# A streaming Huber loss on one core: from bf16 intermediates on three queues to fp32 in place, with every transfer issued by SyncE

## The chip, the cores and the metric

The kernel runs on one core of a Trainium2 chip. The metric is device microseconds of one execution, lower is better. Before the change the median of three runs is 1923.24 us (1923.15 to 1923.33). One further execution was recorded by the hardware profiler; all durations below come from it.

## The reference

Two inputs of 8192x8192 fp32 give one output of the same shape and type:

```python
def reference(pred, target):
    delta = 1.0
    diff = pred - target
    abs_diff = np.abs(diff)
    return np.where(abs_diff <= delta, 0.5 * diff**2, delta * (abs_diff - 0.5 * delta))
```

With c = clip(diff, -1, 1) this is c²/2 + relu(|diff| - 1), which is what both kernels compute. Per element two fp32 numbers are read and one is written: 536.87 MB in and 268.44 MB out.

## The kernel before

The rows are cut into 64 tiles of 128 rows (one row per partition). A tile has 8192 columns, so an input tile is 4 MB (4096 KB), and one tile of work moves 12.58 MB (805.3 MB over 64).

**Loads.** `emit_loads(i)` (lines 46 to 58) loads each input tile in two halves of 4096 columns, 2048 KB and 16 KB rows each. Both halves of `pred` and the first half of `target` are issued from SyncE (SP), the second half of `target` from ScalarE (ACT) (L54, L56). There are three buffers each for `a` (pred) and `b` (target), each half a tile wide.

**Work.** In the main loop (tiles 0 to 61) GpSimd (POOL) subtracts the halves into a bf16 tile `dfull` (L103), ACT takes the absolute value in place (L108), VectorE (DVE) writes min(|d|, 1) into the bf16 tile `sfull` (L109), and one tile later `do_tail` squares `sfull` on ACT with a scale (L68), applies relu(|d| - 1) on ACT (L69) and adds the two on DVE (L70). Each of these but the subtraction is one instruction over 128x8192 elements.

**Stores.** `flush` issues one 4096 KB store per tile from POOL's queue (L63), which turns bf16 into fp32 on the way.

**End.** The last two tiles are cut into pieces of 2048 and 1024 columns (lines 120 to 228). Their pieces use DVE forms that the main loop does not have, among them L147 (scalar_tensor_tensor, two tensors in), L152 (tensor_tensor) and L154 (tensor_scalar) over 128x2048.

**What sets the order.** Each engine runs its own instruction list strictly in order and waits on semaphores. The list is not simply the order of the Python source: the tile framework plans it from dependencies and its own estimates when the program is built. Each load waits on its issuing engine until its buffer is released.

Of the kernel before, what the change touches and what calls it, by code (L numbers as in the profile page):

```python
# [9 lines left out]
def kernel(  # L10
# [6 lines left out]
    nc = tc.nc  # L17
    P = 128
    fp32 = mybir.dt.float32
    bf16 = mybir.dt.bfloat16  # L20
    Alu = mybir.AluOpType
    Act = mybir.ActivationFunctionType

    n_rows, n_cols = pred.shape
    COLS = 4096
    n_ct = n_cols // COLS
    SQRT_HALF = 0.70710678118654752
# [6 lines left out]
    neg1 = nc.alloc_sbuf_tensor("huber_neg1_bf16", [P, 1], bf16)  # L34
# [4 lines left out]
    pool_d = ctx.enter_context(tc.tile_pool(name="sbuf_d", bufs=2))  # L39
    pool_s = ctx.enter_context(tc.tile_pool(name="sbuf_s", bufs=3))  # L40

    loads = {}
    pending_tail = []
    pending_store = []

    def emit_loads(i):
        if i >= n_rt:
            return
        tl = []
        for j in range(n_ct):  # L50
            c0 = j * COLS
            a = pool_a.tile([P, COLS], fp32)
            b = pool_b.tile([P, COLS], fp32)
            nc.sync.dma_start(out=a, in_=pred_t[i, :, c0 : c0 + COLS])  # L54
            beng = nc.sync if j == 0 else nc.scalar
            beng.dma_start(out=b, in_=targ_t[i, :, c0 : c0 + COLS])  # L56
            tl.append((a, b))
        loads[i] = tl

    def flush(limit):  # L60
        while len(pending_store) > limit:
            r, pi = pending_store.pop(0)
            nc.gpsimd.dma_start(out=out_t[pi, :, :], in_=r)  # L63

    def do_tail(limit):
        while len(pending_tail) > limit:
            s, d, pi = pending_tail.pop(0)
            nc.scalar.activation(out=s, in_=s, func=Act.Square, scale=SQRT_HALF)  # L68
            nc.scalar.activation(out=d, in_=d, func=Act.Relu, bias=neg1.ap())  # L69
            nc.vector.tensor_tensor(out=s, in0=s, in1=d, op=Alu.add)  # L70
            pending_store.append((s, pi))

    def act_path(d, s):
        nc.scalar.activation(out=d, in_=d, func=Act.Abs)
        nc.vector.tensor_scalar(
            out=s, in0=d, scalar1=1.0, scalar2=None, op0=Alu.min
        )
        nc.scalar.activation(out=s, in_=s, func=Act.Square, scale=SQRT_HALF)
        nc.scalar.activation(out=d, in_=d, func=Act.Relu, bias=neg1.ap())
        nc.vector.tensor_tensor(out=s, in0=s, in1=d, op=Alu.add)  # L80

    def dve_path(d, s):
        nc.vector.tensor_scalar(
            out=s, in0=d, scalar1=-1.0, scalar2=1.0, op0=Alu.max, op1=Alu.min
        )
        nc.vector.scalar_tensor_tensor(
            out=d, in0=s, scalar=-0.5, in1=d, op0=Alu.mult, op1=Alu.add
        )
        nc.vector.tensor_tensor(out=s, in0=s, in1=d, op=Alu.mult)

    emit_loads(0)
    for i in range(n_rt - 2):
        dfull = pool_d.tile([P, n_cols], bf16)
        sfull = pool_s.tile([P, n_cols], bf16)

        emit_loads(i + 1)

        do_tail(0)

        for j in range(n_ct):  # L100
            c0 = j * COLS
            a, b = loads[i][j]
            nc.gpsimd.tensor_tensor(  # L103
                out=dfull[:, c0 : c0 + COLS], in0=a, in1=b, op=Alu.subtract
            )
        del loads[i]

        nc.scalar.activation(out=dfull, in_=dfull, func=Act.Abs)  # L108
        nc.vector.tensor_scalar(  # L109
            out=sfull, in0=dfull, scalar1=1.0, scalar2=None, op0=Alu.min,  # L110
        )

        flush(1)

        pending_tail.append((sfull, dfull, i))

    i62 = n_rt - 2
    i63 = n_rt - 1
    H = n_cols // 2

    d62 = pool_d.tile([P, n_cols], bf16, tag="dfull")
    s62 = pool_s.tile([P, n_cols], bf16, tag="sfull")

    emit_loads(i63)
    do_tail(0)

    for j in range(n_ct):
        c0 = j * COLS
        a, b = loads[i62][j]
        nc.gpsimd.tensor_tensor(  # L130
            out=d62[:, c0 : c0 + COLS], in0=a, in1=b, op=Alu.subtract
        )
    del loads[i62]

    flush(1)

    Q = 2048
    dq = [d62[:, k * Q : (k + 1) * Q] for k in range(4)]
    sq = [s62[:, k * Q : (k + 1) * Q] for k in range(4)]
    nc.scalar.activation(out=dq[0], in_=dq[0], func=Act.Abs)  # L140
    nc.vector.tensor_scalar(out=sq[0], in0=dq[0], scalar1=1.0, scalar2=None, op0=Alu.min)  # L141
    nc.vector.tensor_scalar(  # L142
        out=sq[1], in0=dq[1], scalar1=-1.0, scalar2=1.0, op0=Alu.max, op1=Alu.min
    )
    nc.scalar.activation(out=sq[0], in_=sq[0], func=Act.Square, scale=SQRT_HALF)  # L145
    nc.scalar.activation(out=dq[0], in_=dq[0], func=Act.Relu, bias=neg1.ap())
    nc.vector.scalar_tensor_tensor(  # L147
        out=dq[1], in0=sq[1], scalar=-0.5, in1=dq[1], op0=Alu.mult, op1=Alu.add
    )
    nc.vector.tensor_tensor(out=sq[0], in0=sq[0], in1=dq[0], op=Alu.add)  # L150
    nc.scalar.activation(out=dq[2], in_=dq[2], func=Act.Abs)
    nc.vector.tensor_tensor(out=sq[1], in0=sq[1], in1=dq[1], op=Alu.mult)  # L152
    nc.vector.tensor_scalar(out=sq[2], in0=dq[2], scalar1=1.0, scalar2=None, op0=Alu.min)  # L153
    nc.vector.tensor_scalar(  # L154
        out=sq[3], in0=dq[3], scalar1=-1.0, scalar2=1.0, op0=Alu.max, op1=Alu.min
    )
    nc.scalar.activation(out=sq[2], in_=sq[2], func=Act.Square, scale=SQRT_HALF)  # L157
    nc.scalar.activation(out=dq[2], in_=dq[2], func=Act.Relu, bias=neg1.ap())  # L158
    nc.vector.scalar_tensor_tensor(  # L159
        out=dq[3], in0=sq[3], scalar=-0.5, in1=dq[3], op0=Alu.mult, op1=Alu.add  # L160
    )
    nc.vector.tensor_tensor(out=sq[2], in0=sq[2], in1=dq[2], op=Alu.add)  # L162
    nc.vector.tensor_tensor(out=sq[3], in0=sq[3], in1=dq[3], op=Alu.mult)

    d63 = pool_d.tile([P, n_cols], bf16, tag="dfull")
    s63 = pool_s.tile([P, n_cols], bf16, tag="sfull")

    bounds = [0, 2048, 4096, 6144, 7168, 8192]
    chunks = [(bounds[k], bounds[k + 1]) for k in range(len(bounds) - 1)]

    flush(0)
    for k, (lo, hi) in enumerate(chunks):
        a, b = loads[i63][lo // COLS]
        o0, o1 = lo % COLS, (hi - 1) % COLS + 1
        nc.gpsimd.tensor_tensor(  # L175
            out=d63[:, lo:hi], in0=a[:, o0:o1], in1=b[:, o0:o1], op=Alu.subtract
        )
        if 1 <= k <= 4:
            nc.gpsimd.dma_start(  # L179
                out=out_t[i62, :, (k - 1) * Q : k * Q], in_=sq[k - 1]  # L180
            )
    del loads[i63]

    d0, s0 = d63[:, 0:2048], s63[:, 0:2048]
    d1, s1 = d63[:, 2048:4096], s63[:, 2048:4096]
    d2, s2 = d63[:, 4096:6144], s63[:, 4096:6144]
    d3, s3 = d63[:, 6144:7168], s63[:, 6144:7168]
    d4, s4 = d63[:, 7168:8192], s63[:, 7168:8192]

    def st(lo, hi, s):  # L190
        nc.gpsimd.dma_start(out=out_t[i63, :, lo:hi], in_=s)  # L191

    nc.scalar.activation(out=d0, in_=d0, func=Act.Abs)
    nc.vector.tensor_scalar(out=s0, in0=d0, scalar1=1.0, scalar2=None, op0=Alu.min)  # L194
    nc.scalar.activation(out=s0, in_=s0, func=Act.Square, scale=SQRT_HALF)  # L195
    nc.scalar.activation(out=d0, in_=d0, func=Act.Relu, bias=neg1.ap())
    nc.vector.tensor_scalar(
        out=s1, in0=d1, scalar1=-1.0, scalar2=1.0, op0=Alu.max, op1=Alu.min
    )
    nc.vector.scalar_tensor_tensor(  # L200
        out=d1, in0=s1, scalar=-0.5, in1=d1, op0=Alu.mult, op1=Alu.add
    )
    nc.vector.tensor_tensor(out=s1, in0=s1, in1=d1, op=Alu.mult)
    st(2048, 4096, s1)
    nc.vector.tensor_tensor(out=s0, in0=s0, in1=d0, op=Alu.add)
    st(0, 2048, s0)
    nc.scalar.activation(out=d2, in_=d2, func=Act.Abs)
    nc.vector.tensor_scalar(out=s2, in0=d2, scalar1=1.0, scalar2=None, op0=Alu.min)
    nc.scalar.activation(out=s2, in_=s2, func=Act.Square, scale=SQRT_HALF)
    nc.scalar.activation(out=d2, in_=d2, func=Act.Relu, bias=neg1.ap())  # L210
    nc.vector.tensor_scalar(
        out=s4, in0=d4, scalar1=-1.0, scalar2=1.0, op0=Alu.max, op1=Alu.min
    )
    nc.vector.scalar_tensor_tensor(
        out=d4, in0=s4, scalar=-0.5, in1=d4, op0=Alu.mult, op1=Alu.add
    )
# [40 lines left out]
```

## Time and profile before

| Quantity | Value |
|---|---|
| median of three runs | 1923.24 us |
| span of the profiled execution | 1921.5 us |
| median less that span (the time around it) | 1.74 us |
| data moved over the span | 805.42 MB, mean 419 GB/s |
| DVE busy | 851.1 us (44%) |
| ACT busy | 1326.3 us (69%) |
| POOL busy | 1289.1 us (67%) |

"Busy" counts an engine's own work. The span runs from the first to the last instruction. A group row reads: line, engine, operation, tiles and shapes, count, then busy time in us and the mean duration of one in ns. A timeline row reads: start in us, duration in us, engine, line, operation. The windows view gives busy time of each engine in a stretch, and for the transfers their busy share (over 1.00 where packets of two queues overlap on an engine) and GB/s.

### The profile page before, as it was taken

What the parts mean: (1) busy time and instruction counts of PE and PEld (TensorE: products, weight loads), DVE (VectorE), ACT (ScalarE), POOL (GpSimd) and SP (SyncE); (2) the same over time, 40 slices, a digit from 0 to 9 for tenths busy, and PEclk for the clock granted to TensorE, in tenths of its full rate; (3) what the DMA queues carried; (4) which work ended last, traced back from release to release, by engine and by line L of the source; (5) the groups of instructions that cost most, each with busy time, mean ns of one, the idle gap of its engine ahead of it and who ended that gap; (6) DMA issues with size and microseconds to landing.
All of it is one profiled execution on the core that took longest, in us unless ns stands there. A gap on an engine that the chain in (4) does not pass through costs nothing.

```text
span 1921.5 us, 1430 instructions
## 1 busy us (share of the span) xinstructions
DVE 851.1 (44%) x146; ACT 1326.3 (69%) x202; POOL 1289.1 (67%) x207
## 2 busy tenths in 40 slices
DVE  0344354453443534534435345344353443544566
ACT  2866767668677676686776866767768667676674
POOL 5686676766866767667677676676766866767664
DMA  9999999999999999999999999999999999999996
GB/s 404 378 415 426 425 428 425 422 424 426 424 426 424 426 423 426 423 427 424 427 422 425 424 426 422 428 424 425 422 425 427 424 424 423 425 424 424 426 432 269
DMA packets 47099, 805.42 MB, mean 419 GB/s; under 512 B 5232, under 2 KB 5232, under 8 KB 5488
## 3 DMA queue, kind: packets, MB, share of 16 engines
q1 hardware_dynamic: 27648, 402.67, 54.0%
q0 software_dynamic: 10224, 268.44, 32.9%
q10 hardware_dynamic: 9216, 134.22, 16.3%
q14 instruction: 11, 0.09, 0.0%
HBM read 536.87 MB, written 268.44 MB: 419 GB/s over the span
## 4 chain that ended last, share of the span: by engine, by line
ACT 51%; DVE 29%; issue 18%; DMA 1%; POOL 1%; ACTq 0%; POOLq 0%; SPq 0%
DVE sfull L109 28%; ACT dfull L108 23%; ACT sfull L68 22%; ACT dfull L69 5%; DMA b<-in_target_dram 1%; POOL dfull L103 1%; DVE s_1188 L153 1%; DVE s_1188 L142 0%; DVE sfull L70 0%; DVE s_1220 L194 0%; DVE d_1187 L147 0%; DVE d_1187 L159 0%; ACT d_1187 L158 0%; ACT s_1220 L195 0%; ACTq L252 0%
## 5 line engine op out<-in xcount | busy, mean ns | idle before, releaser
L103 POOL TENSOR_TENSOR dfull<-a,b 128x4096 bf16<-128x4096 f32 x124 | 1213.8, 9803 | 588.0 <-issue 558.8
L68 ACT ACTIVATE sfull<-sfull 128x8192 bf16<-128x8192 bf16 x62 | 435.9, 7030 | 532.8 <-DVE sfull L109 532.8
L70 DVE TENSOR_TENSOR sfull<-sfull,dfull 128x8192 bf16<-128x8192 bf16 x62 | 274.4, 4426 | 860.6 <-ACT dfull L69 860.6
L109 DVE TENSOR_SCALAR sfull<-dfull 128x8192 bf16<-128x8192 bf16 x62 | 528.7, 8528 | 194.9 <-ACT dfull L108 194.9
L108 ACT ACTIVATE dfull<-dfull 128x8192 bf16<-128x8192 bf16 x62 | 434.8, 7013 | 33.2 <-POOL dfull L103 33.2
L69 ACT ACTIVATE dfull<-dfull,huber_neg_bf 128x8192 bf16<-128x8192 bf16 x62 | 440.6, 7106 | 0.0
L63 POOL DMA_DIRECT2D out_dram<-sfull x62 | 35.8, 577 | 3.8 <-DVE sfull L70 3.8
L130 POOL TENSOR_TENSOR d_1187<-a,b 128x4096 bf16<-128x4096 f32 x2 | 19.6, 9836 | 9.5 <-issue 9.5
L175 POOL TENSOR_TENSOR d_1219<-a,b 128x2048 bf16<-128x2048 f32 (+1 forms) x5 | 18.1, 3643 | 0.1
L191 POOL DMA_DIRECT2D out_dram<-s_1220 x5 | 2.7, 541 | 11.7 <-DVE s_1220 L217 5.9
L153 DVE TENSOR_SCALAR s_1188<-d_1187 128x2048 bf16<-128x2048 bf16 x1 | 9.8, 9846 | 0.0
L142 DVE TENSOR_SCALAR s_1188<-d_1187 128x2048 bf16<-128x2048 bf16 x1 | 9.3, 9318 | 0.0
L179 POOL DMA_DIRECT2D out_dram<-s_1188 x4 | 2.2, 553 | 10.5 <-DVE s_1188 L152 4.2
L195 ACT ACTIVATE s_1220<-s_1220 128x2048 bf16<-128x2048 bf16 x1 | 1.9, 1910 | 8.1 <-DVE s_1220 L194 8.1
L162 DVE TENSOR_TENSOR s_1188<-s_1188,d_1187 128x2048 bf16<-128x2048 bf16 x1 | 6.1, 6057 | 2.7 <-ACT d_1187 L158 2.7
L157 ACT ACTIVATE s_1188<-s_1188 128x2048 bf16<-128x2048 bf16 x1 | 1.9, 1910 | 6.0 <-DVE s_1188 L153 6.0
L145 ACT ACTIVATE s_1188<-s_1188 128x2048 bf16<-128x2048 bf16 x1 | 1.9, 1910 | 4.1 <-DVE s_1188 L141 4.1
L194 DVE TENSOR_SCALAR s_1220<-d_1219 128x2048 bf16<-128x2048 bf16 x1 | 3.3, 3278 | 0.0
L147 DVE SCALAR_TENSOR_TENSOR d_1187<-s_1188,d_1187 128x2048 bf16<-128x2048 bf16 x1 | 2.3, 2293 | 0.0
L159 DVE SCALAR_TENSOR_TENSOR d_1187<-s_1188,d_1187 128x2048 bf16<-128x2048 bf16 x1 | 2.3, 2284 | 0.0
L200 DVE SCALAR_TENSOR_TENSOR d_1219<-s_1220,d_1219 128x2048 bf16<-128x2048 bf16 x1 | 2.3, 2280 | 0.0
L108 ACT ACT_TABLE_LOAD x1 | 1.3, 1283 | 1.2 <-PEq L241 1.2
(32 smaller groups left out, 34.7 us busy)
## 6 DMA issues: line engine op xcount, KB each, us to landing
a<-in_pred_dram SPq DMA_DIRECT2D x128, 2048.0 KB, 18.1
out_dram<-sfull POOLq DMA_DIRECT2D x62, 4096.0 KB, 20.1
b<-in_target_dram ACTq DMA_DIRECT2D x64, 2048.0 KB, 13.9
b<-in_target_dram SPq DMA_DIRECT2D x64, 2048.0 KB, 25.3
out_dram<-s_1188 POOLq DMA_DIRECT2D x4, 1024.0 KB, 7.9
out_dram<-s_1220 POOLq DMA_DIRECT2D x3, 1024.0 KB, 4.1
out_dram<-s_1220 POOLq DMA_DIRECT2D x2, 512.0 KB, 5.0
```

The costliest lines, as they stand in the source:

```text
L63: nc.gpsimd.dma_start(out=out_t[pi, :, :], in_=r)
L68: nc.scalar.activation(out=s, in_=s, func=Act.Square, scale=SQRT_HALF)
L69: nc.scalar.activation(out=d, in_=d, func=Act.Relu, bias=neg1.ap())
L70: nc.vector.tensor_tensor(out=s, in0=s, in1=d, op=Alu.add)
L103: nc.gpsimd.tensor_tensor(out=dfull[:, c0 : c0 + COLS], in0=a, in1=b, op=Alu.subtract)
L108: nc.scalar.activation(out=dfull, in_=dfull, func=Act.Abs)
L109: nc.vector.tensor_scalar(out=sfull, in0=dfull, scalar1=1.0, scalar2=None, op0=Alu.min,)
L130: nc.gpsimd.tensor_tensor(out=d62[:, c0 : c0 + COLS], in0=a, in1=b, op=Alu.subtract)
L142: nc.vector.tensor_scalar(out=sq[1], in0=dq[1], scalar1=-1.0, scalar2=1.0, op0=Alu.max, op1=Alu.min)
L153: nc.vector.tensor_scalar(out=sq[2], in0=dq[2], scalar1=1.0, scalar2=None, op0=Alu.min)
L162: nc.vector.tensor_tensor(out=sq[2], in0=sq[2], in1=dq[2], op=Alu.add)
L175: nc.gpsimd.tensor_tensor(out=d63[:, lo:hi], in0=a[:, o0:o1], in1=b[:, o0:o1], op=Alu.subtract)
```

## The change

The intermediates in bf16, the POOL work and the separate tiles `dfull` and `sfull` go. There are three slots each for `a` and `b`, each a whole fp32 tile of 128x8192 (rows of 32 KB), and all work is done in place in them:

- `load(i)` issues one 4096 KB load for `a` and one for `b`, `store(i)` one 4096 KB store of `b`, all from SP, in the fixed order: loads of tile i, then the store of tile i-2. Only the last tile's `target` load and store are cut into four of 1024 KB. The store moves fp32 to fp32.
- `chunk` treats 2048 columns at a time, four per tile: DVE subtracts into `a` (L68), DVE clips into `b` (L69), ACT squares `b` with the scale (L72), takes the absolute value of `a` (L73) and relu(|d| - 1) of `a` (L74). `add` (L65) adds `a` into `b` on DVE; the source calls it two chunks later.
- A load of tile i+3 can only start when its slots are free: `a` when tile i's last add is done, `b` when tile i's store has landed.

```diff
+    CH = 2048
+    n_ch = n_cols // CH
-    pool_d = ctx.enter_context(tc.tile_pool(name="sbuf_d", bufs=2))
-    pool_s = ctx.enter_context(tc.tile_pool(name="sbuf_s", bufs=3))
+    def load(i):
+        a = pool_a.tile([P, n_cols], fp32)
+        nc.sync.dma_start(out=a, in_=pred_t[i, :, :])
+        b = pool_b.tile([P, n_cols], fp32)
+        pieces = n_ch if i == n_rt - 1 else 1
+        w = n_cols // pieces
+        for k in range(pieces):
+            nc.sync.dma_start(
+                out=b[:, k * w : (k + 1) * w], in_=targ_t[i, :, k * w : (k + 1) * w]
+            )
+        return a, b
+    def store(i, b):
+        pieces = n_ch if i == n_rt - 1 else 1
+        w = n_cols // pieces
+        for k in range(pieces):
+            nc.sync.dma_start(
+                out=out_t[i, :, k * w : (k + 1) * w], in_=b[:, k * w : (k + 1) * w]
+            )
+    flight = []
+    def add(a, b):
+        nc.vector.tensor_tensor(out=b, in0=b, in1=a, op=Alu.add)
+    def chunk(a, b):
+        nc.vector.tensor_tensor(out=a, in0=a, in1=b, op=Alu.subtract)
         nc.vector.tensor_scalar(
-            out=s, in0=d, scalar1=1.0, scalar2=None, op0=Alu.min
+            out=b, in0=a, scalar1=-1.0, scalar2=1.0, op0=Alu.max, op1=Alu.min
         )
+        nc.scalar.activation(out=b, in_=b, func=Act.Square, scale=SQRT_HALF)
+        nc.scalar.activation(out=a, in_=a, func=Act.Abs)
+        nc.scalar.activation(out=a, in_=a, func=Act.Relu, bias=neg1.ap())
+        flight.append((a, b))
+        if len(flight) > 2:
+            add(*flight.pop(0))
+    tiles = {}
+    for i in range(n_rt + 2):
+        if i < n_rt:
+            tiles[i] = load(i)
+        if i == n_rt:
+            while flight:
+                add(*flight.pop(0))
+        if i >= 2:
+            store(i - 2, tiles.pop(i - 2)[1])
+        if i < n_rt:
+            a, b = tiles[i]
+            for k in range(n_ch):
+                sl = slice(k * CH, (k + 1) * CH)
+                chunk(a[:, sl], b[:, sl])
...
-    emit_loads(0)
-    for i in range(n_rt - 2):
...
```

When the program is built, the planner fixes the lists of the engines. From the fourth tile to the last they repeat, per tile (chunks 0 to 3):

```
DVE: L68 c0, L68 c1, L69 c0, L69 c1, L68 c2, L68 c3, L69 c2, L69 c3, L65 c0, L65 c1, L65 c2, L65 c3
ACT: L72 c0, L73 c0, L72 c1, L74 c0, L73 c1, L72 c2, L74 c1, L73 c2, L72 c3, L74 c2, L73 c3, L74 c3
```

In tiles 0 to 2 the lists of neighbouring tiles are interleaved: on DVE the first clip of tile 1 stands behind the third add of tile 0, and the subtractions of tile 2 behind the third add of tile 1.

More of the change, by code (lines that the diff above doesn't have):

```diff
@@ L19 @@
     fp32 = mybir.dt.float32
-    bf16 = mybir.dt.bfloat16
     Alu = mybir.AluOpType
     Act = mybir.ActivationFunctionType
+    SQRT_HALF = 0.70710678118654752
     n_rows, n_cols = pred.shape
-    COLS = 4096
-    n_ct = n_cols // COLS
-    SQRT_HALF = 0.70710678118654752
+    CH = 2048
+    n_ch = n_cols // CH
     pred_t = pred.rearrange("(n p) m -> n p m", p=P)
@@ L32 @@
     n_rt = pred_t.shape[0]
-    neg1 = nc.alloc_sbuf_tensor("huber_neg1_bf16", [P, 1], bf16)
+    neg1 = nc.alloc_sbuf_tensor("huber_neg1", [P, 1], fp32)
     nc.gpsimd.memset(neg1.ap(), -1.0)
@@ L38 @@
     pool_b = ctx.enter_context(tc.tile_pool(name="sbuf_b", bufs=3))
-    pool_d = ctx.enter_context(tc.tile_pool(name="sbuf_d", bufs=2))
-    pool_s = ctx.enter_context(tc.tile_pool(name="sbuf_s", bufs=3))
[L42 to L71, printed above, removed]
@@ L73, in act_path @@
-    def act_path(d, s):
-        nc.scalar.activation(out=d, in_=d, func=Act.Abs)
+    def load(i):
[9 more added lines that the diff above has]
+        return a, b
@@ L77, in act_path @@
         )
[L78 to L89, printed above, removed]
@@ L91 @@
-    emit_loads(0)
-    for i in range(n_rt - 2):
[L93 to L216, printed above, removed]
-    nc.vector.tensor_tensor(out=s2, in0=s2, in1=d2, op=Alu.add)
@@ L218 @@
-    st(4096, 6144, s2)
-    nc.scalar.activation(out=d3, in_=d3, func=Act.Abs)
-    nc.vector.tensor_scalar(out=s3, in0=d3, scalar1=1.0, scalar2=None, op0=Alu.min)
-    nc.scalar.activation(out=s3, in_=s3, func=Act.Square, scale=SQRT_HALF)
-    nc.scalar.activation(out=d3, in_=d3, func=Act.Relu, bias=neg1.ap())
-    nc.vector.tensor_tensor(out=s4, in0=s4, in1=d4, op=Alu.mult)
-    st(7168, 8192, s4)
-    nc.vector.tensor_tensor(out=s3, in0=s3, in1=d3, op=Alu.add)
-    st(6144, 7168, s3)
+        nc.scalar.activation(out=b, in_=b, func=Act.Square, scale=SQRT_HALF)
```

## The prediction

> **What bounds the kernel now.** I read the page's busy line and its slices of transfer first, then windows, then the tail of the timeline for the prices of single instructions.
>
> ```profile
> span 1921.5 us, 1430 instructions
> DVE 851.1 (44%) x146; ACT 1326.3 (69%) x202; POOL 1289.1 (67%) x207
> ...
> DMA  9999999999999999999999999999999999999996
> GB/s 404 378 415 426 425 428 425 422 424 426 424 426 424 426 423 426 423 427 424 427 422 425 424 426 422 428 424 425 422 425 427 424 424 423 425 424 424 426 432 269
> ```
>
> No engine is busy over 69%; the transfers are busy in every slice. Windows: a stretch at the start with loads alone, 31 periods of the main loop, the end.
>
> ```profile
> 0.00:5.00 5.00, 0.00 (x0) 1.28 (x1) 0.31 (x5) 1.00 0.66 229
> 5.00:30.00 25.00, 0.00 (x0) 0.00 (x0) 11.94 (x2) 1.00 1.01 432
> 103.70:1022.33 918.63, 403.94 (x63) 649.83 (x93) 624.98 (x94) 1.00 1.04 425
> 1882.00:1921.50 39.50, 24.64 (x15) 17.83 (x11) 16.09 (x11) 1.00 0.61 234
> ```
>
> The last two columns are the transfers' busy share and GB/s. The main loop takes 918.63/31 = 29.63 us per tile for 12.58 MB, with the transfers at share 1.04: transfers set its pace. Loads alone, nearly all on one queue, reach 432 GB/s. The end loses: 39.5 us at 234 instead of 425 GB/s is 18 us lost.
>
> ```profile
> 1863.46 2.29 DVE L147 SCALAR_TENSOR_TENSOR d_1187<-s_1188,d_1187 128x2048 bf16<-128x2048 bf16 x1
> 1865.67 0.69 DVE L154 TENSOR_SCALAR s_1188<-d_1187 128x2048 bf16<-128x2048 bf16 x1
> 1866.27 1.22 DVE L152 TENSOR_TENSOR s_1188<-s_1188,d_1187 128x2048 bf16<-128x2048 bf16 x1
> ...
> 1896.10 3.28 DVE L194 TENSOR_SCALAR s_1220<-d_1219 128x2048 bf16<-128x2048 bf16 x1
> ...
> 1899.41 1.91 ACT L195 ACTIVATE s_1220<-s_1220 128x2048 bf16<-128x2048 bf16 x1 [8.13 <-DVE s_1220 L194]
> 1901.23 1.99 ACT L196 ACTIVATE d_1219<-d_1219,huber_neg_bf 128x2048 bf16<-128x2048 bf16 x1
> ...
> 1903.12 1.89 ACT L207 ACTIVATE d_1219<-d_1219 128x2048 bf16<-128x2048 bf16 x1
> ...
> 1904.92 1.04 ACT L219 ACTIVATE d_1219<-d_1219 128x1024 bf16<-128x1024 bf16 x1
> ```
>
> To be seen: prices at 2048 columns, and start to start. Square to relu 1.82 us, relu to abs 1.89, abs to next 1.80 (an independent successor starts about 0.1 before the end). On DVE L147 to L154 is 2.21 for a 2.29. DVE to ACT costs 0.03 (L194 ends 1899.38, L195 starts 1899.41).
>
> **Part 1, transfers.** Bytes are the same. Removed: POOL's converting stores and ACT's loads; five transfers per tile become three. Bounds per tile: 12.58/0.432 = 29.1 us (loads alone), 12.58/0.425 = 29.6 (the mixed loop). I take 29.4: the new queue also holds one kind at a time, but a third of it is stores, whose plain fp32 form no row shows; the converting stores ran inside the 425. Transfers alone would thus give 2.3 us lost at the start (5 us at 229 instead of 432 GB/s is 2.35), 64 x 29.4 = 1881.6, and an end of 5 us after the last byte, 1889 us of span. That would be faster.
>
> Size gains nothing here: two loads of 2 MB in a row already run at 432 GB/s. The Trainium skill, DMA: Bandwidth & Descriptors, section "Anatomy of one DMA — SWDGE (gpsimd) path", gives about 2.0 us fixed plus bytes at 436 GB/s per transfer. If that were paid in series, two transfers fewer would save an estimated 4 us per tile; the 432 GB/s window shows that queued transfers hide it.
>
> **Part 2, the loop through DVE and ACT.** The compiled lists decide this. From the fourth tile on, DVE does a tile's four adds directly ahead of the next tile's first subtraction, although the source calls them two chunks later. The last add waits for ACT's last relu of that tile; ACT's first square of the next tile waits for that tile's first clip, which stands behind two subtractions. So one tile's chain is closed before the next begins, whatever is already loaded:
>
> - two subtractions, start to start 2 x 2.21 = 4.42;
> - one clip 1.22, and 0.03 to ACT: ACT starts at 5.67;
> - ACT: four squares, abs and relus, 4 x (1.82 + 1.80 + 1.89) = 22.04. The last relu stands directly behind the abs that it needs and cannot overlap it: 0.12 more; its full 1.99 counts: 0.10 more. ACT ends at 27.93;
> - 0.03 to DVE, and the last add, start to start 2.21: 30.17; my count with the overlaps that the rows give is 30.1.
>
> Everything else (clips and subtractions of chunks 2 and 3, adds 0 to 2) lies beside ACT, whose 22.04 us cover them: 4.42 + 3 x 1.14 + 3 x 2.21 = 14.5 us of DVE. If that cover went, DVE's whole 4 x (2.21 + 1.14 + 2.21) = 22.2 us would still be under 29.4.
>
> Unseen prices. fp32 subtract and add on DVE: the bf16 tensor_tensor is 1.22 (L152), the only fp32 row is POOL's L175, 4.5 us at 2048 columns. I take 2.29: L147 also reads two tensors at one element per step, and 1.22 with twice the bytes less its fixed 0.16 (1.22 against 0.69 at 1024, L223) comes to 2.28. At 1.22 the loop would be 26.9, under the transfers; at 4.5 it would be 36.8. fp32 clip: between 0.69 (L154, bf16) and 2.29 (L147); by bytes 0.69 x 2 less 0.16 is 1.22, the value taken. At 0.69 the loop is 29.6, at 2.29 it is 31.2. ACT in fp32: its time grows by 0.83 ns per element from 2048 (1.91) to 8192 (7.03), and DVE's L152 takes bytes out of the same memory faster, so elements and not bytes set it; unchanged is the value, twice is the far end (by bytes, 52 us a tile), a gain I exclude since fewer bytes did not make the bf16 pace.
>
> The Trainium skill, VectorE: DVE Perf Modes, section "The perf-mode tier table (the rule you actually need)", prices fp32 tensor_tensor at 2293 ns and fp32 tensor_scalar at 1227 ns for 2048 elements, twice their bf16 prices: a rule against this change. By its figures the loop is an estimated 30.1 to 30.2, as by the rows; at the rows' far ends it is 26.9 or 36.8. No row of this trace shows either form.
>
> **Part 3, the waits on SP.** SP issues load i, then store i-2; a waiting store holds the later loads. After tile j's last add, SP issues store j and the load of `a` for j+3; the load of `b` waits for store j to land: 9.8 us of transfer and some 2 to land, while `a` itself takes 9.8 behind the store. Then `b` is in about 31 us after the add; tile j+3 begins two loops, 60 us, after it. This costs nothing while the loop is the longer. If it is not, the cover is `a`'s 9.8 us against a landing of 2. POOL's work goes: 67% busy, off the path. With it goes DVE's slow clip beside POOL (8.53 us, against 3.85 in the first tile, at 42.72): L109 is in the chain of work with 28%, but the transfers set that pace, so I price it at nothing.
>
> **Part 4, start and end.** Tile 0 is complete at about 22.2 (2.35 + 8.39 MB at 0.432 = 21.8, plus an estimated 0.4 until the semaphore is seen). ACT starts 5.67 later, at 27.9, and runs through tiles 0 and 1 without a hole, since the planner mixes them: 22.1 for tile 0, 22.6 for tile 1, whose four relus each stand directly behind their abs (22.04 + 4 x 0.12 + 0.10), so to 72.6. Tile 2's subtractions start behind tile 1's third add, which follows its third relu at 67.0: at 69.2. Tile 2 ends at 69.2 + 30.1 = 99.3. Then 61 tiles at 30.1 follow: 1835.4 (61 x 30.09), last add at 1935. After it the last 1024 KB store: before, from the last store's issue at 1912.66 to the end were 8.8 us (bounds: landings took 4.1 to 5.1; the rest is closing), so 1944 of span. The end no longer loses 18 us of transfer, but the chain, not transfers, ends last.
>
> **Sum.** 99.3 + 1835.4 + 8.8 = 1943.5, rounded up to 1944 of span, against the profiled 1921.5. Around it lie 1923.24 - 1921.5 = 1.74 us. Predicted: 1946 us, 1.2% slower.
>
> **Rivals.**
> - *Transfers set the pace, faster.* If ACT does not go empty between tiles (a chip order or prices that close the chain under 29.4), the time is 1889 + 1.7 = 1891. It decides from a loop of 30.1 - 23/61 = 29.7 on, only 0.4 us under mine. For it: DVE and ACT need only 22 us each. Against: the lists are fixed, and ACT's 22.04 are measured. With a clip of 0.69 alone: 29.6 x 61 gives 1914.
> - *The clip or the chain is dearer.* A clip of 2.29 lengthens the loop by 1.07 and the first tiles by 7.7: 1946 + 65 + 7 = 2018. For it: no fp32 clip is shown. Against: the bytes.
> - *One ring cannot keep the pace.* With loads and stores in one order, each change of kind could leave a gap. From 0.7 us per tile on it decides (12.58 MB in 30.1 is 418 GB/s); 1 us per transfer gives 29.4 + 3 = 32.4 x 64 + 10 = 2084. Against: 432 GB/s across several loads in a row.
> - *The change does less than it says.* A 32 KB row may still be cut into smaller packets; with 16 KB rows already at 432 GB/s this is worth nothing.
>
> **How the numbers follow.** Chances: my loop 0.73 (its own range 1932 to 1962, a quarter microsecond a tile either way), transfers pacing or a cheap clip 0.13, a dear clip 0.09, the ring 0.05. Leaving out the 1891 case, the 2084 case and the end of the dear clip gives 1910 to 1985, about 8 in 10. A measurement of this kernel tells 0.2% from no change, that is 1919.4 to 1927.1. Slower: 0.73 + 0.09 + 0.05 less a sliver, 0.85; the same 0.03; faster 0.12.
>
> **What would show it.** Right: ACT busy about 22 x 64 = 1400 us, idle some 8 us once per tile before the square, waiting for the clip; the last add waiting for ACT; transfers near 418 GB/s with SP waiting on DVE; clip rows of 1.2 us. Wrong: transfers at 425 or more throughout and SP stalled only on landings (the first rival); clip rows near 2.3; fp32 subtraction rows far from 2.29; or ACT rows over 2 us, which would make all of it longer.

## The result, and the profile after

The changed kernel takes 1943.91 us (median of four, 1943.79 to 1943.94) against 1923.20 us for the kernel before: a ratio of 1.0108, 95% interval 1.0093 to 1.0122. It is slower, by about 20.7 us. The profiled execution has a span of 1942.2 us.

The page of the changed kernel: head, GB/s in 40 equal slices of the span, shares of the chain of work that ended last, groups:

```profile
span 1942.2 us, 2040 instructions
...
DVE 1435.1 (74%) x768; ACT 1421.5 (73%) x769; POOL 0.3 (0%) x5
...
GB/s 413 429 431 432 431 433 432 431 434 435 432 433 430 427 413 420 423 411 421 421 410 422 420 411 422 418 422 412 416 421 415 421 420 411 421 420 421 411 367 173
...
ACT 73%; DVE 19%; issue 7%; DMA 1%; DVEq 0%; SPq 0%
...
L65 DVE TENSOR_TENSOR b<-b,a 128x2048 f32<-128x2048 f32 x256 | 586.2, 2290 | 479.4 <-ACT a L74 479.4
L72 ACT ACTIVATE b<-b 128x2048 f32<-128x2048 f32 x256 | 485.8, 1898 | 488.5 <-DVE b L69 488.5
L68 DVE TENSOR_TENSOR a<-a,b 128x2048 f32<-128x2048 f32 x256 | 574.4, 2284 | 22.9 <-DMA b<-in_target_dram 22.9
L74 ACT ACTIVATE a<-a,huber_neg 128x2048 f32<-128x2048 f32 x256 | 509.5, 1990 | 2.2
L73 ACT ACTIVATE a<-a 128x2048 f32<-128x2048 f32 x256 | 484.7, 1894 | 0.0
L69 DVE TENSOR_SCALAR b<-a 128x2048 f32<-128x2048 f32 x256 | 301.7, 1219 | 0.0
```

Three readings matter. First, the idle columns: ACT's square (L72) waited 488.5 us for DVE's clip, and DVE's add (L65) waited 479.4 us for ACT's relu. The two engines wait for each other. Neither is busy over 74%, and DVE waited for a load only once, 22.9 us at the very start. Second, the chain that ended last: 73% of the span are ACT's work, 19% DVE's, 1% transfers. Third, the GB/s row: up to the 13th slice the transfers run at about 432 GB/s, and SP waits almost only for landings of stores (280 us between 100 and 400 us, against 22 us for DVE's adds); from the 15th on they fall to 410 to 423, because they are now held back to the pace of the work (between 1000 and 1900 us SP waits 525 us for the adds, 328 for landings).

One period of the loop, in the timeline of the changed kernel (start, duration, engine, line):

```profile
911.00 2.29 DVE L65 TENSOR_TENSOR b<-b,a 128x2048 f32<-128x2048 f32 x1 [1.54 <-ACT a L74]
913.22 4.49 DVE L68 TENSOR_TENSOR a<-a,b 128x2048 f32<-128x2048 f32 x2
...
917.62 2.35 DVE L69 TENSOR_SCALAR b<-a 128x2048 f32<-128x2048 f32 x2
918.87 1.91 ACT L72 ACTIVATE b<-b 128x2048 f32<-128x2048 f32 x1 [7.90 <-DVE b L69]
...
939.09 2.00 ACT L74 ACTIVATE a<-a,huber_neg 128x2048 f32<-128x2048 f32 x1
941.12 2.29 DVE L65 TENSOR_TENSOR b<-b,a 128x2048 f32<-128x2048 f32 x1 [1.54 <-ACT a L74]
943.33 2.28 DVE L68 TENSOR_TENSOR a<-a,b 128x2048 f32<-128x2048 f32 x1
```

To be seen: the period is 943.33 - 913.22 = 30.11 us. From the first subtraction to ACT's first square 5.65 us, ACT from 918.87 to 941.09, 22.22 us without a hole, then 0.03 and the last add's 2.21 until the next tile's subtraction can start. ACT stands idle 7.90 us once per tile, between its last relu and the next tile's first clip, though the next tile's data is there: after the start DVE waits for no load.

What SP waited for, in the changed kernel (who waited, for whom, us in total, times, longest; L46 issues the load of `b`, L55 the store):

```profile
SPq L46 <- DMA out_dram<-b: 917.6, 61, 28.1
SPq L55 <- DVE b L65: 916.5, 65, 32.0
```

These are the two longest waits of the whole trace and cost nothing here, as the experiment with half the stores shows below: SP waits because it is early.

The transfers' busy share does not show who sets the pace. A late stretch in the changed kernel, and then the same in the source-order kernel below, which does wait for its loads (the last two columns are busy share and GB/s):

```profile
1022.00:1850.00 828.00, 615.40 (x329) 608.48 (x330) 0.00 (x0) 1.00 1.00 418
```

```profile
1022.00:1850.00 828.00, 645.37 (x343) 643.14 (x342) 0.00 (x0) 1.00 1.00 431
```

Both have 1.00: in the changed kernel, whose transfers are held back, some packet records are longer (a 32 KB row takes 1239 ns in the mean against 1217 in the source-order run, with a median of 1213 in both). So the share of 1.04 in the kernel before does not by itself show that transfers set its pace, as the prediction reads it; no run tested that.

The kernel before spends 29.63 us per tile, this one 30.12 ((1907.14 - 100.01)/60 from the first subtractions of the last and the fourth tile). Over 61 periods that is 30 us more; some 9 us of it come back at the two ends, which I did not separate.

### The profile page after: what moved, and what is told of

It is laid out like the page before. It is cut to its first block, busy times and chain, and to the rows that moved or that the text cites. A ratio compares the mean times of both kernels' runs of the same rounds, so it can differ in the third digit from the quotient of the medians.

```text
span 1942.2 us, 2040 instructions
## 1 busy us (share of the span) xinstructions
DVE 1435.1 (74%) x768; ACT 1421.5 (73%) x769; POOL 0.3 (0%) x5
## 4 chain that ended last, share of the span: by engine, by line
ACT 73%; DVE 19%; issue 7%; DMA 1%; DVEq 0%; SPq 0%
ACT a L74 25%; ACT b L72 24%; ACT a L73 24%; DVE a L68 15%; DVE b L69 4%; DMA b<-in_target_dram 1%; DVE b L65 0%; DVEq L69 0%; SPq L41 0%; DVEq L68 0%
## 5 line engine op out<-in xcount | busy, mean ns | idle before, releaser
L65 DVE TENSOR_TENSOR b<-b,a 128x2048 f32<-128x2048 f32 x256 | 586.2, 2290 | 479.4 <-ACT a L74 479.4
L72 ACT ACTIVATE b<-b 128x2048 f32<-128x2048 f32 x256 | 485.8, 1898 | 488.5 <-DVE b L69 488.5
L68 DVE TENSOR_TENSOR a<-a,b 128x2048 f32<-128x2048 f32 x256 | 574.4, 2284 | 22.9 <-DMA b<-in_target_dram 22.9
L74 ACT ACTIVATE a<-a,huber_neg 128x2048 f32<-128x2048 f32 x256 | 509.5, 1990 | 2.2
L73 ACT ACTIVATE a<-a 128x2048 f32<-128x2048 f32 x256 | 484.7, 1894 | 0.0
L69 DVE TENSOR_SCALAR b<-a 128x2048 f32<-128x2048 f32 x256 | 301.7, 1219 | 0.0
```

What stands on the lines that cost most here:

```text
L65: nc.vector.tensor_tensor(out=b, in0=b, in1=a, op=Alu.add)
L68: nc.vector.tensor_tensor(out=a, in0=a, in1=b, op=Alu.subtract)
L69: nc.vector.tensor_scalar(out=b, in0=a, scalar1=-1.0, scalar2=1.0, op0=Alu.max, op1=Alu.min)
L72: nc.scalar.activation(out=b, in_=b, func=Act.Square, scale=SQRT_HALF)
L73: nc.scalar.activation(out=a, in_=a, func=Act.Abs)
L74: nc.scalar.activation(out=a, in_=a, func=Act.Relu, bias=neg1.ap())
```

## The experiments

### The order of DVE and ACT alone

The edit leaves work, transfers and buffers as they are and only asks the planner to keep the order of the source on DVE and ACT:

```diff
+    keep = tc.keep_in_program_order
-        nc.vector.tensor_tensor(out=b, in0=b, in1=a, op=Alu.add)
+        keep(nc.vector.tensor_tensor(out=b, in0=b, in1=a, op=Alu.add))
-        nc.vector.tensor_tensor(out=a, in0=a, in1=b, op=Alu.subtract)
+        keep(nc.vector.tensor_tensor(out=a, in0=a, in1=b, op=Alu.subtract))
...
```

The clip and ACT's three instructions are wrapped in the same way.

> Same work, transfers and waits as the changed kernel, but DVE and ACT keep the order of the source: a tile's last two adds come after the first two subtractions and clips of the next tile. Theory (the closed chain subtract, subtract, clip, ACT, add sets 30.1 us a tile): the chain opens, DVE needs 4 x (2.32 + 1.14 + 2.21) = 22.7 and ACT 4 x (1.82 + 1.92 + 1.89) = 22.5 us a tile, so transfers pace it at the 431 to 436 GB/s of the changed kernel's early slices: 12.58/0.432 = 29.1 a tile, 1870 to 1890 us in all, faster than the kernel before (1923). Rival (one ring with loads and stores in turn gives only the 412 to 420 GB/s of the later slices): 1925 to 1945, as the changed kernel.

Measured: 1875.21 us, ratio to the kernel before 0.975 (0.9734 to 0.9767); 68.7 us less than the changed kernel. The slices and waits of this run, whose lines stand one further down (L69 subtracts, L70 clips, L73 squares, L75 is the relu, L66 the add):

```profile
span 1873.9 us, 2040 instructions
...
GB/s 414 425 435 430 432 432 433 430 435 432 432 435 432 432 434 432 432 434 434 430 434 435 429 434 434 430 433 434 432 432 434 431 432 432 431 435 432 413 433 367
```

```profile
DVE a L69 <- DMA b<-in_target_dram: 409.2, 62, 22.8
ACT b L73 <- DVE b L70: 385.2, 61, 7.9
...
DVE b L66 <- ACT a L75: 1.4, 1, 1.4
```

The GB/s row no longer falls. DVE now waits for a load on nearly every tile (409.2 us, 62 times) and for ACT once, 1.4 us: the transfers set the pace. (ACT still waits for the clip, 385.2 us, because the clip waits for the load.) The theory holds, and the rival that one ring (a single queue, here SP's) with loads and stores in turn is limited to 412 to 420 GB/s falls. This version beats both kernels.

### One clip moved forward

Here the adds still stand ahead of the next tile; only the subtractions of chunks 1 to 3 are held behind the clip of chunk 0, which `first` keeps. (The planner then moved two more things, as the trace shows: the first add ahead of the fourth subtraction, and ACT's relu of chunk 0 ahead of its square of chunk 1.)

```diff
+        if k >= 1:
+            with tc.issue_after(first[-1].ins):
+                nc.vector.tensor_tensor(out=a, in0=a, in1=b, op=Alu.subtract)
```

> Only one thing of DVE's order is changed: the clip of a tile's first chunk stands directly behind its subtraction, ahead of the subtractions of the other chunks. Adds still come ahead of the next tile. Theory: the chain loses one subtraction, 30.1 - 2.2 + 0.1 = 28.0 us, which is under the transfers' 29.1, so transfers take over and it ends where the source order does plus the last tile's tail, 1870 to 1895 us. If each microsecond of chain counted without a floor it would be 1943 - 2.1 x 61 = 1815. Rival (ring): 1925 to 1945.

Measured: 1876.57 us, ratio 0.9758 (0.9743 to 0.9773). The waits of this run (L74 is the first subtraction):

```profile
DVE a L74 <- DMA b<-in_target_dram: 65.6, 50, 22.8
```

Shortening the chain by one subtraction is enough: DVE now waits for a load 50 times. The gain stops at the transfers, as expected, and not at the 1815 us that the chain alone would give.

### The same dose in two places

A second, idle clip per tile: once for chunk 0, where it stands in the chain, once for chunk 3, where it stands beside ACT. The twin has `k == 3` in the same place. ACT's order of squares and abs is pinned so that the planner does not rearrange it.

```diff
+        if k == 0:
+            nc.vector.tensor_scalar(
+                out=b, in0=b, scalar1=-1.0, scalar2=1.0, op0=Alu.max, op1=Alu.min
+            )
```

> The changed kernel with a second, idle clip for the first chunk of every tile; on DVE it stands behind the clip of the second chunk, so ACT's first square waits 2 x 1.14 = 2.28 us longer. ACT keeps its order. Theory (closed chain): period 30.12 + 2.28 = 32.40, 61 periods give 139 us more, 2075 to 2090 us. Rival (DVE's or ACT's total work, or transfers, set the period): DVE has 7 us of holes per tile, so no change, 1944.

> The same second clip, but for the last chunk of every tile, where it stands behind the first add, ahead of a hole of DVE. The same DVE work is added as in the twin. Theory (closed chain): it lies beside ACT and costs nothing, 1940 to 1950 us. Rival (total work of DVE counts): as much as the twin, 2010 to 2090 us.

Measured: 2084.08 us in the chain (ratio 1.0837, 1.0815 to 1.0858), 1944.36 us beside it (ratio 1.0110, 1.0090 to 1.0130). The first run's line of waits for ACT and the second's (L78 squares, L70 clips, L74 is the second clip):

```profile
ACT b L78 <- DVE b L74: 629.0, 64, 10.2
```

```profile
ACT b L78 <- DVE b L70: 488.1, 63, 7.9
```

In the chain, ACT's wait grows from 7.9 to 10.2 us per tile, by the expected 2.28 of two clips (the second clip of chunk 0, and chunk 1's, behind which it stands); beside ACT it stays. The same added DVE work costs 140 us in one place and 0.5 in the other. Total work does not set the time, the closed chain does.

### Half the stores

```diff
-        w = n_cols // pieces
+        w = n_cols // pieces if i == n_rt - 1 else n_cols // 2
```

> Stores of all tiles but the last cover only columns 0 to 4095; the rest of the output is not written. All compute stays. One sixth of the bytes goes. Theory (chain): no change against the changed kernel, 1940 to 1946 us, period 30.1. Rival (transfers or landings of stores set the pace, since the loads of b wait 918 us in total for stores): down by up to a sixth of the transfers, 1640 to 1900 us.

Measured: 1936.44 us, ratio 1.0069 (1.0054 to 1.0084). A sixth of the bytes less, and 7.5 us less: neither the 0 to 4 of the theory nor anything like the rival's 44 to 300. The transfers are at share 0.85 in the middle of this run, SP's wait for landings of stores falls from 917.6 to 54.3 us, and the period stays: subtractions start at 913.22 and 943.34, as in the changed kernel to 0.01 us. The 7.5 us are at the end:

```profile
1895.64 2.29 DVE L65 TENSOR_TENSOR b<-b,a 128x2048 f32<-128x2048 f32 x1 [2.95 <-ACT a L74]
1897.85 2.29 DVE L68 TENSOR_TENSOR a<-a,b 128x2048 f32<-128x2048 f32 x1
1901.13 2.29 DVE L65 TENSOR_TENSOR b<-b,a 128x2048 f32<-128x2048 f32 x1 [1.00 <-ACT a L74]
1903.34 1.22 DVE L69 TENSOR_SCALAR b<-a 128x2048 f32<-128x2048 f32 x1
```

In this build the planner put the last tile's first subtraction and clip ahead of the last adds of the tile before. One of the 61 places where the chain closes between two tiles is gone (ACT waits 62 times instead of 63), and each costs 7.9 us of ACT's time. So the run misses its expectation by a change of order that I had not looked for, and that change is a small copy of the first experiment.

### Transfers by themselves

All compute left out; the stores write the loaded target.

```diff
-                chunk(a[:, sl], b[:, sl])
+                pass
```

> All compute is left out; what is stored is the loaded target. The loads and stores, their order and their slots stay. It prices the transfers by themselves. Theory: 805.3 MB at 432 GB/s is 1864, with start and end 1870 to 1880 us. Rival (ring slower by itself): 1925 or more.

Measured: 1870.53 us, ratio 0.9727 (0.9707 to 0.9746). One ring moves loads and stores in turn at 432 to 433 GB/s (windows 103 to 1022 and 1022 to 1850 us). The source-order kernel is 4.7 us above this floor.

### Stores from POOL's queue, and rows of 16 KB

Both start from the source-order kernel and undo one part of the change in its transfers. The first issues the stores, in `store`, from POOL:

```diff
-            nc.sync.dma_start(
+            nc.gpsimd.dma_start(
                 out=out_t[i, :, k * w : (k + 1) * w], in_=b[:, k * w : (k + 1) * w]
             )
```

> The source-order kernel with its stores issued from POOL's queue instead of SP's; still fp32 to fp32, no conversion. It undoes one part of the change and asks what raised the transfers from 425 GB/s (kernel before) to 432. Theory: the stores' own path through POOL cost it; with it the main loop falls back to 425 GB/s, 1900 to 1910 us. Rival (the path is free; the conversion, or 16 KB rows, or the mixing by two more queues cost it): 1873 to 1880 us.

The second loads `a`, and `b` in the same way, in halves:

```diff
-        nc.sync.dma_start(out=a, in_=pred_t[i, :, :])
+        for k in range(2):
+            nc.sync.dma_start(
+                out=a[:, k * 4096 : (k + 1) * 4096],
+                in_=pred_t[i, :, k * 4096 : (k + 1) * 4096],
+            )
```

> The source-order kernel with every load of a and b cut into two halves of 4096 columns, 16 KB rows and 2048 KB each, as the kernel before had them; all still from SP. In the traces a 16 KB row takes 611 ns on its transfer engine (kernel before), a 32 KB row 1213 (source-order run). Theory (the row length itself has a price): 32 x 611 - 16 x 1213 = 0.14 us a tile, and two more transfers with their completions, estimated from nothing to 0.1; 64 tiles give 9 to 16 us, 1884 to 1891 us. Rival (row length is free, POOL's queue made all the difference): 1875 to 1877 us.

Measured: 1905.05 us with POOL's stores (1898.99 to 1906.36; ratio 0.9898, 0.9879 to 0.9916), 1885.43 us with halves (ratio 0.9801, 0.9783 to 0.9818). So stores from POOL's queue cost 30 us (24 to 31 over the four runs) and loads in halves 10 us against 1875.21. The windows of the POOL run (us, busy of DVE, ACT and POOL, clock, transfers' share, GB/s):

```profile
103.00:1022.00 919.00, 714.80 (x381) 712.66 (x379) 17.05 (x32) 1.00 1.00 429
1022.00:1850.00 828.00, 626.27 (x333) 626.25 (x333) 14.39 (x27) 1.00 1.00 424
```

Against 432 and 431 in the same windows of the source-order run. The 10 us fit the packet records: a 16 KB row takes 611 ns (median) on its transfer engine in the kernel before and 612 in this run, a 32 KB row 1213, so 32 x 611 - 16 x 1213 = 144 ns a tile (176 with 612), 9 to 11 us over 64. Halves are also twice as many loads; the packets alone account for the difference, but rows and number of loads were not tried apart.

For POOL's queue the median packet shows no price: there too a 32 KB row takes 1213 ns. By the windows about 20 of the 30 us are lost in the loop: (919 x 3 + 828 x 7)/431. There a few of SP's load packets are longer: 470 of 16256 take over 1.6 us, against 79 of 24320 in the source-order run, and the mean is 1237 against 1217 ns, which over 1016 packets on each transfer engine is some 20 us too. After the last landing the span goes on for 3.6 us instead of 1.0. What makes those packets longer (POOL's issue, the turn between two queues, or a queue that stands empty while SP waits) was not tried and stays open.

### The end

From the source-order kernel again, in `store`:

```diff
-        pieces = n_ch if i == n_rt - 1 else 1
+        pieces = n_ch if i >= n_rt - 2 else 1
```

> The source-order kernel with the store of the last tile but one cut into four pieces as well, so that its first pieces need not wait for the adds that stand behind the last tile's first chunks. In the source-order run the transfers fall to 365 GB/s between 1840 and 1850 us. Theory: that hole of some 2 us closes, 1871 to 1874 us. Rival (the hole is from semaphores shared with the last loads): no change, 1875.

Measured: 1874.61 us (1873.30 to 1875.58), ratio 0.9747 (0.9732 to 0.9761): not to be told from the source-order kernel's 0.975. Between 1840 and 1850 us the transfers rise from 365 to 408 GB/s, between 1850 and 1860 they are at 386 instead of 398. Much of the hole closes, and nothing is gained: it was not on the path. In the source-order run DVE gets its last long-awaited load, that of the last tile but one, at 1814.74; from there the chain that ended last holds only work of DVE and ACT, up to the end of the last add at 1866.03, and 7.9 us follow. With the cut store it is 1814.11, 1865.41 and 7.9: the same 51.3 us of work. So the theory failed. The rival's number came true, but its reason was not tested.

## Why the prediction was right

The predicted 1946 us is 2 us above the measured 1943.9, and the loop came about as it was worked out. That the total is so near is partly luck, since errors at the start and the end partly cancel.

- **Part 2, the closed chain: right, in each term.** Lead-in to ACT 5.67 predicted, 5.65 measured; ACT 22.26 (to 27.93), measured 22.22; hop and last add 2.24, measured 2.24; the loop 30.1 by the count with overlaps, 30.12 on average. The prices that the trace before did not show came out at the value taken: subtraction 2.284 and add 2.290 (taken 2.29), clip 1.219 (taken 1.22), ACT in fp32 1.898, 1.894 and 1.990 as in bf16. Against the bf16 rows of the trace before (1.22 and 0.69) the fp32 forms cost 1.87 and 1.77 times, a little under the prediction's "twice". The Trainium skill, VectorE: DVE Perf Modes, section "The perf-mode tier table (the rule you actually need)", has 2293 and 1227 ns for the two DVE forms; the groups above agree to 0.7%.
- **Part 4, start and end: misses that partly cancel.** Tile 0 was complete at 22.86 instead of 22.2, tile 2 began at 69.89 instead of 69.2, the fourth tile at 100.01 instead of 99.3: 0.7 us late throughout, and with the loop's hundredths (61 x 0.03) the last add ended at 1937.3 instead of 1934.7 (99.3 + 1835.4). The end after it took 4.9 us (1942.2 - 1937.3), not 8.8: the 1024 KB stores from SP landed in 3.8 us (median) where POOL's took up to 5.1, and from the last landing to the end of the span it was 1.0 us instead of 3.7. The term was 3.9 too large.
- **Part 3, SP's waits: right.** They are long and idle. Half the stores took 863 us of waiting for landings away and left the period as it was.
- **Part 1, transfers: right that they do not decide, wrong in two of its statements.** "I take 29.4" per tile, 1889 us of span, was too high: the transfers alone have a span of 1868.8, that is the lower end of 29.1 per tile. And "Size gains nothing here" failed: loads in halves, with 16 KB rows, cost 10 us once transfers set the pace. I had read 432 GB/s as a ceiling for both sizes from a window of 25 us, where a difference of 0.7% cannot be seen. Taking the stores off POOL's queue, which I priced only as part of the 425 GB/s, is worth 30 us. Neither shows in the changed kernel, because its chain is longer than its transfers.
- **The rivals.** "Transfers set the pace, faster" was the right account of what lies under the chain: opened by order (1875.2) or shortened by one instruction (1876.6), the kernel goes there; its price of 1891 was 16 us too high, mainly by the same 29.4. The dear clip and the ring fell: 1.219 us, and 432 GB/s in one ring.

Where did the change's gain go? Its transfers alone are done in 1870.5 us, some 50 us under the kernel before; the loads' halves are worth 10 of them and the stores' queue 30, by the two runs that undo them one at a time; whether the two add up, and what the rest is, was not tried. The planner's order gave 68.7 us back, by closing a chain of 30.12 us per tile where the transfers need 29.1. ACT's idle time alone does not tell: in the source-order run it still waits 385.2 us for clips, but there behind the loads.

## What to carry to other kernels

Before reading busy shares, read the compiled order of the engines: two engines at 74% each can be a closed loop. In this one, 2.28 us of clips between one engine's last result and the other's first input counted in full, and a clip beside the other engine counted nothing. A planned order need not be the order written; where the source interleaves two tiles on purpose, pin that order. And when transfers set the pace, fewer queues and longer rows are worth measuring even if a short window shows the same GB/s.

## What the runs showed of the hardware that I had not expected

- The queue that issues a plain fp32 store matters: 30 us in 1875 between SP and POOL, with the same median packet (1213 ns). The Trainium skill, DMA: Bandwidth & Descriptors, section "Rules for kernel authors", says that spreading transfers over several issuing engines does not help bandwidth; here it did worse than not help, 429 and 424 GB/s against 432 and 431.
- A row of 32 KB costs 1213 ns, two of 16 KB 1222. This difference of 0.7% comes to 9 of the 10 us of the run with halves.
- Loads and stores in turn in one ring run as fast as loads alone: 432 to 433 GB/s over 1747 us, against 432 in the window of loads of the kernel before (which is only 25 us long, and has rows of 16 KB).
- A busy share of 1.00 was recorded for transfers that were held back to 418 GB/s as well as for transfers that set the pace at 431.
